# S5 tables in another layout, weights rounded one unit earlier, and other planner costs in a one-core decoder trunk

## The chip, the cores and the metric

The kernel runs on one core of a Trainium2 chip. The metric is device time in microseconds (us), the median of three runs. TensorE (PE) does the matmuls, VectorE (DVE), ScalarE (ACT) and GpSimd (POOL) the rest, and SyncE (SP) issues most DMAs. POOL and ACT issue DMAs too, in order with their other instructions.

## The reference

One decoder layer over 512 tokens of width 1024, in float32. Three token mixers run side by side on the normalised input: a gated linear recurrence (LRU, branch a), chunked gated linear attention (GLA, branch b) and a complex diagonal state space (S5, branch c). They are merged by sigmoid gates; cross attention to 256 memory tokens and a SwiGLU follow, each with a residual and a layer norm.

```python
proj = h @ w_in + b_in
u_lru, g_lru, q, k, v, og, lr, u_s5, gate_logits = jnp.split(proj, IN_SPLITS, axis=-1)
y_a = rg_lru(causal_dwconv(u_lru, ...), ...) * gelu(g_lru)
y_b = rms_norm(gla_chunked(q, k, v, log_f), gla_norm_g) * silu(og)
z = gelu(s5_ssm(u_s5, ...)); y_c = z * sigmoid(z @ s5_w_glu + s5_b_glu)
gates = sigmoid(gate_logits.reshape(B_, L, N_BRANCH, D_MODEL))
merged = sum(gates * einsum('blnw,nwd->blnd', ys, w_branch), axis=2)
h = layer_norm(DN_ALPHA * h + merged @ w_mix_out, ln1_g, ln1_b)
h = layer_norm(DN_ALPHA * h + cross_attention(h, mem, ...), ln2_g, ln2_b)
h = layer_norm(DN_ALPHA * h + swiglu(h, w_gu, w_down), ln3_g, ln3_b)
# s5_ssm, for 32 groups of 16 channels with 64 complex states each:
mag = exp(lam_re * dt); ab = mag * (cos(lam_im * dt) + i sin(lam_im * dt))
x[t] = ab * x[t-1] + (f * b) u[t];   y[t] = Re(c x[t]) + d u[t]
```

## The kernel before

**Tiles.** Activations lie transposed, features on the 128 partitions and all 512 tokens along a row; a `heap` tile is 128x512 float32 (52 buffers). Each matmul is done in three passes to keep float32 accuracy: the weight is split into a rounded half `whi` (ACT copies `raw` to fp32r) and a remainder `wlo` (DVE, `raw - whi`), the activation likewise into `..h` and `..l`, and `mm3` multiplies hi by hi, hi by lo and lo by hi. A weight unit is 128x1024 (512 KB), 162 of them are split so; one unit makes eight contraction blocks, 24 matmuls of 512 columns. `take(name)` (L248) hands out the next unit, splits units up to three ahead (`split_to`, L225) and issues DMAs three further (`dma_to`, L216). Raw and split units share one pool of 14 buffers.

**Stages.** Input layer norm (`ln_in`, L465) and the keys `kT`; the projections `us` (S5 input), `u`, `g`, `qk`, `lr`, `vo`; then, between the gate units `gt` and the branch projections `br`, the three mixers; `w_mix` and layer norm 1 (`proj_ln`, L1284); the memory values `xv` and queries `xq`; the heads (L1379); `w_xo` and layer norm 2; the first feed-forward units `f0` (first the tokens 0 to 255 of four units, then 256 to 511 of the same four); `fg`, `fu`; `w_dn` and layer norm 3.

**Order.** The program is written out when the kernel is built. Each engine runs its own list in order. Main work (projections) is straight code. The mixers, the layer norms of the token tiles and the heads are generators in the background (`start_bg`, L302). At each `slot()` (L278) the planner lets a generator write its next step if the clocks it keeps for DVE and ACT are less than `LEAD` ns ahead of its clock for PE, and if the tiles that the step names are ready by its own account (`_account`, L77). What an instruction costs in that account is in `pe_cost`, `dve_cost`, `act_cost`, `pool_cost` (L98 to L125). So these estimates decide the order of the instructions on every engine, and nothing else. A generator may hold at most three PSUM banks (`hold`, L263).

**S5.** `s5_prep` (L601) builds tables on POOL: the powers 0 to 7 of `ab` (`pw`), ordered by power and then group, the scaled `bb` and `bbs`, the eighth power of the phase (`wr`, `wi`), and `bz`. For each quarter q of the groups, `phasors(q)` (L716) makes the 64 phases per group (`phr`, `phi`) on POOL by doubling: five squarings of 128x8 (`sq`) and five complex products growing to 128x256. `s5a` (L753) has DVE make two `E` and two `C` stacks (each two products and a sum, the second product in `tm`), PE transpose `E` into `Et` and multiply `C` by `bz` into `G`, ACT copy `G` into `gx`, and POOL's DMA queue load `U` and route `gx` through memory into `Tz`. `s5b` then does `e = Et U` on PE, eight small matmuls put one by one behind the threes of the main work (`pump`), DVE's scan, and `y`. The merge of a branch is DVE's `th<-th,br`, which reads the branch's PSUM bank; the next use of the bank waits for it.

**Layer norm of a tile.** When `p` of a token tile is done, DVE adds the residual, ACT sums squares, POOL takes the power -1/2 (`st<-st,mh`), DVE scales (`lh`); PE transposes (`tp`), ACT and DVE round into `h1Th`, `h1Tl`. `xq` needs those of all four tiles.

Of the kernel before, what the change touches and what calls it, by code (L numbers as in the profile page):

```python
# [16 lines left out]
P = 128  # L17
# [22 lines left out]
AHEAD = 3  # L40
DMA_AHEAD = 3
NHEAP = 52
LOG = []
LEAD = 6500.0
# [7 lines left out]
class Plan:  # L52


    def __init__(self):
        self.written, self.read, self.dma = {}, {}, 0.0
# [5 lines left out]
class Engine:  # L62
# [14 lines left out]
    def _account(self, name, a, k):  # L77
        aps = [x for x in (*a, *k.values()) if hasattr(x, "free_size")]
        outs, ins = [aps[0]] + [x for x in [k.get("accum_out")] if x is not None], aps[1:]
        p = self._plan  # L80
        t = self.ns
        for x in ins:
            t = max(t, p.written.get(x.name, 0.0) + (HOP if name != "matmul" else 0.0))
# [3 lines left out]
        end = t + self._cost(self, name, a, k, aps)  # L87
        self.ns = end
# [9 lines left out]
def pe_cost(eng, name, a, k, aps):  # L98
    if name == "transpose":
        return 109.0  # L100
    rhs = k["rhs"]
    return rhs.free_size() / 2.4 if rhs.dtype == F32R else max(rhs.free_size() / 0.6, 110.0)


def dve_cost(eng, name, a, k, aps):
    n = max(x.free_size() for x in aps[:2])
    return 67.0 + n * {"memset": 0.5, "reciprocal": 6.0}.get(name, 1.0) / 0.96


def act_cost(eng, name, a, k, aps):  # L110
    if name != "activation":
        return 700.0
    ns = 60.0 + 0.83 * aps[0].free_size() + (200.0 if "accum_out" in k else 0.0)
    func = a[2]
    if func not in (AF.Copy, AF.Identity, AF.Square, AF.Abs) and func != eng.func:
        eng.func = func
        ns += 1300.0
# [3 lines left out]
def pool_cost(eng, name, a, k, aps):  # L121
    return 1100.0 if name == "dma_start" else 100.0 + 0.9 * aps[0].free_size()
# [7 lines left out]
def hybrid_kernel(ctx: ExitStack, tc: tile.TileContext, I, out, dbg=None):  # L130
# [17 lines left out]
    def H(s, dt=F32):  # L148
        return heap.tile([P, 512], dt, tag="h", name=nm(s))
# [64 lines left out]
    st = {"dma": 0, "split": 0}  # L214
# [10 lines left out]
    def split_to(n):  # L225
        while st["split"] < min(n, len(order)):
            i = st["split"]
            dma_to(i + 1)
            if i < NK32:
                st["split"] += 1  # L230
                continue
            name, _, size = order[i]
            if name == "w_lr":
# [3 lines left out]
                split(p3[:, 0], p3[:, 1], r3)  # L237
                splits[i] = pair
                st["split"] += 1
                continue  # L240
            hi, lo = W("whi", F32R), W("wlo", F32R)
            split(hi[:, :size], lo[:, :size], raws.pop(i)[:, :size])
            splits[i] = (hi, lo)
            st["split"] += 1
# [3 lines left out]
    def take(name, ahead=AHEAD):  # L248
# [3 lines left out]
        split_to(i + 1 + ahead)  # L252
        dma_to(min(st["split"], i + 1 + AHEAD) + DMA_AHEAD)
# [347 lines left out]
    def s5_prep(R):  # L601
# [978 lines left out]
```

## Time and profile before

| | |
|---|---|
| median of three runs | 1030.89 us (1029.96 to 1031.49) |
| profiled execution | 1030.58 us |
| its span | 1028.9 us |
| mean granted clock of PE | 0.986 |
| PE busy | 995.0 us, 97% |
| DVE, ACT, POOL busy | 539.4, 367.3, 232.9 us |

The span runs from the first to the last instruction that the profile shows; 1.7 us lie outside it. PE is busy nearly always, so what can be won without taking matmuls away is its idle time and the time in which it ran at the lower of its two clocks (1.2 instead of 2.4 GHz).

### The profile page before, as it was taken

The page shows a single profiled execution, that of the slowest core. Times are in us where ns is not written, and L with a number is a line of the kernel's source. Part 1 is how long each engine was busy: PE and PEld are TensorE (multiplying, and loading weights), DVE is VectorE, ACT ScalarE, POOL GpSimd, SP SyncE. Part 2 cuts the span into 40 slices and gives each one's busy share as a digit, 9 for nine tenths or more (in the row PEclk, how much of TensorE's full clock was granted, in tenths as well). Part 3 has the DMA queues.
Part 4 walks back from the last instruction along what each step waited for, and adds up shares of the span by engine and source line. Part 5 has one row for each costly group of instructions (what it writes and reads, how often), then busy time and mean ns, then how long its engine had stood idle before and what let it go on. Part 6 is the DMA issues. An engine that isn't in the chain of part 4 may idle for free. (4 is left out here: it accounts for less than half of the span.)

```text
span 1028.9 us, 12601 instructions
## 1 busy us (share of the span) xinstructions
PE 995.0 (97%) x4856; PEld 822.4 (80%) x4856; DVE 539.4 (52%) x857; ACT 367.3 (36%) x598; POOL 232.9 (23%) x465
## 2 busy tenths in 40 slices
PE   9999979998989799999999999999999999999996
PEld 7888757876878688888888887898888888888885
DVE  5625846887294654457594555833333332242316
ACT  5634357422233232553343443433322312331211
POOL 1489950083745700002010000200000000000001
PEclk9999989999999899999999999999999999999999
DMA  9932243212342344537232311353342222232202
GB/s 351 333 135 87 85 124 103 82 62 83 103 123 103 116 144 161 169 110 230 95 131 96 123 42 62 110 198 110 126 123 98 97 102 103 93 112 93 92 20 83
DMA packets 38365, 123.76 MB, mean 120 GB/s; under 512 B 4865, under 2 KB 5281, under 8 KB 38305
## 3 DMA queue, kind: packets, MB, share of 16 engines
q1 hardware_dynamic: 29856, 97.79, 27.4%
q0 software_dynamic: 6592, 22.02, 6.8%
q10 hardware_dynamic: 1856, 3.15, 1.1%
q8 instruction: 38, 0.62, 0.3%
q14 instruction: 23, 0.18, 0.1%
HBM read 109.31 MB, written 11.53 MB: 117 GB/s over the span
## 5 line engine op out<-in xcount | busy, mean ns | idle before, releaser
L73 DVE TENSOR_TENSOR wlo<-raw,whi 128x1024 fp32r<-128x1024 f32 x162 | 197.9, 1228 | 220.7 <-ACT whi L73 165.0
L73 ACT ACTIVATE whi<-raw 128x1024 fp32r<-128x1024 f32 x162 | 168.4, 1055 | 63.7 <-DVE wlo L73 42.4
L73 PE MATMUL p<-whi,act 128*128 128x512 f32 x352 | 108.6, 389 | 0.0
L73 POOL TENSOR_TENSOR st<-st,mh 128x1 f32<-128x1 f32 x16 | 15.5, 970 | 396.2 <-DVE st L73 396.2
L73 PE MATMUL gt<-h0Th,whi 128*128 128x512 f32 x192 | 79.6, 415 | 7.8 <-DVE th L73 7.8
L73 PEld LDWEIGHTS p<-whi,act 128*128 128x128 f32 x352 | 66.1, 188 | 13.7
L73 PE MATMUL gt<-h0Tl,whi 128*128 128x512 f32 x192 | 76.5, 398 | 0.0
L73 PE MATMUL gt<-h0Th,wlo 128*128 128x512 f32 x192 | 76.3, 397 | 0.0
L73 PE MATMUL p<-wlo,act 128*128 128x512 f32 x176 | 68.5, 389 | 0.0
L73 PE MATMUL fg<-h2Th,whi 128*128 128x512 f32 x160 | 62.3, 389 | 0.0
L73 PE MATMUL fg<-h2Tl,whi 128*128 128x512 f32 x160 | 62.3, 389 | 0.0
L73 PE MATMUL fg<-h2Th,wlo 128*128 128x512 f32 x160 | 62.2, 389 | 0.0
L73 PE MATMUL fu<-h2Th,whi 128*128 128x512 f32 x160 | 62.2, 389 | 0.0
L73 PE MATMUL fu<-h2Tl,whi 128*128 128x512 f32 x160 | 62.2, 389 | 0.0
L73 PE MATMUL fu<-h2Th,wlo 128*128 128x512 f32 x160 | 62.2, 389 | 0.0
L73 ACT ACTIVATE th<-gt,gbh 128x512 f32<-128x512 f32 x24 | 16.5, 688 | 121.1 <-PE gt L73 100.5
L73 PEld LDWEIGHTS gt<-h0Th,whi 128*128 128x128 f32 x192 | 37.1, 193 | 14.7 <-DVE th L73 8.0
L73 ACT ACTIVATE sl<-fg 128x512 f32<-128x512 f32 x20 | 12.0, 598 | 99.4 <-PE fg L73 99.4
L73 PEld LDWEIGHTS gt<-h0Th,wlo 128*128 128x128 f32 x192 | 37.0, 193 | 8.1
L73 PEld LDWEIGHTS gt<-h0Tl,whi 128*128 128x128 f32 x192 | 37.1, 193 | 6.5
L73 DVE TENSOR_TENSOR sl<-sl,fu 128x512 f32<-128x512 f32 x20 | 13.7, 687 | 52.7 <-PE fu L73 52.7
L73 PE MATMUL p<-whi,oT 128*128 128x512 f32 x128 | 40.6, 391 | 0.0
(349 smaller groups left out, 2224.1 us busy)
## 6 DMA issues: line engine op xcount, KB each, us to landing
raw<-in_w_gu SPq DMA_DIRECT2D x44, 512.0 KB, 3.3
raw<-in_w_dn SPq DMA_DIRECT2D x22, 512.0 KB, 3.2
raw<-in_w_xk SPq DMA_DIRECT2D x8, 512.0 KB, 6.8
raw<-in_w_gatea SPq DMA_DIRECT2D x8, 512.0 KB, 3.2
raw<-in_w_gateb SPq DMA_DIRECT2D x8, 512.0 KB, 3.5
raw<-in_w_gatec SPq DMA_DIRECT2D x8, 512.0 KB, 3.3
raw<-in_w_xv SPq DMA_DIRECT2D x8, 512.0 KB, 4.3
raw<-in_w_mix SPq DMA_DIRECT2D x8, 512.0 KB, 3.9
```

The costliest lines, as they stand in the source:

```text
L73: return f(*a, **k)
```

## The change

Three things are changed.

1. *S5 tables.* `pw` and the stacks are ordered by group, then channel, then power, so that DVE's products write rows without a stride; before they wrote with a stride of eight elements. `phasors(q)` is no longer a doubling: once, two tables of eight powers per group are made for all 32 groups (`tables`: eight squarings of 128x32 and four complex products of 128x64 or 128x128), and a quarter is their outer product, six operations of 128x512 and the sign. `bz` is made per quarter by DVE (a memset and two copies), not by POOL.
2. *Weights.* `whi` of a unit is written one unit earlier than its `wlo` (`EARLY`), by `hi_to`.
3. *Planner.* The cost estimates are others, `LEAD` is 7000 ns.

The diff, cut to what is spoken of below:

```diff
@@ -38,10 +38,11 @@
 NBUF_W = 14
 NPAIR = 5
 AHEAD = 3
+EARLY = 1
 DMA_AHEAD = 3
 NHEAP = 52
 LOG = []
-LEAD = 6500.0
+LEAD = 7000.0
 NWARM = 2
...
-            t = max(t, p.written.get(x.name, 0.0) + (HOP if name != "matmul" else 0.0))
+            t = max(t, p.written.get(x.name, 0.0) + HOP)
...
-            end = p.dma + 1800.0
+            end = p.dma + (2000.0 if len(aps[0].ap) < 3 and len(aps[1].ap) < 3 else 4000.0)
+        elif name in ("matmul", "transpose"):
+            end += 165.0
...
+    n = rhs.free_size()
+    return n / 2.4 + 13.0 if rhs.dtype == F32R else max(n / 0.6 + 26.0, 180.0)
...
-    return 67.0 + n * {"memset": 0.5, "reciprocal": 6.0}.get(name, 1.0) / 0.96
...
+    return (n + 151.0) / 0.96 + (180.0 if "accum_out" in k else 0.0)
...
+
+    def hi_to(n):
+
+        while st["hi"] < min(n, len(order)):
+            i = st["hi"]
             dma_to(i + 1)
+            st["hi"] += 1
             if i < NK32:
-                st["split"] += 1
                 continue
...
+                hi = W("whi", F32R)
+                his[i] = (hi[:, :size], None, raws.pop(i)[:, :size], hi)
+            A.activation(his[i][0], his[i][2], AF.Copy)

+    def split_to(n):
+        while st["split"] < min(n, len(order)):
+            i = st["split"]
+            hi_to(i + 1)
+            st["split"] += 1
...
+            V.tensor_tensor(lo, raw, hi.bitcast(F32), ALU.subtract)
...
+        hi_to(i + 1 + ahead + EARLY)
...
-        pr, pi = (pw[0][:, 256 * m:256 * m + 256].rearrange("p (d g) -> p d g", g=32) for m in range(2))
-        pt = w[:, 384:512].rearrange("p (d g) -> p d g", g=32)
-        E.tensor_copy(pr[:, 0], abr)
-        E.tensor_copy(pi[:, 0], abi)
+        pr, pi = (pw[0][:, 256 * m:256 * m + 256].rearrange("p (g d) -> p g d", d=8) for m in range(2))
+        pt = w[:, 384:512].rearrange("p (g d) -> p g d", d=4)
+        E.tensor_copy(pr[:, :, 0], abr)
+        E.tensor_copy(pi[:, :, 0], abi)
         for k in (1, 2, 4):
-            s4 = [P, k, 32]
-            cmul(pr[:, k:2 * k], pi[:, k:2 * k], pr[:, 0:k], pi[:, 0:k],
-                 pr[:, k - 1:k].to_broadcast(s4), pi[:, k - 1:k].to_broadcast(s4), pt[:, 0:k])
+            s4 = [P, 32, k]
+            cmul(pr[:, :, k:2 * k], pi[:, :, k:2 * k], pr[:, :, 0:k], pi[:, :, 0:k],
+                 pr[:, :, k - 1:k].to_broadcast(s4), pi[:, :, k - 1:k].to_broadcast(s4), pt[:, :, 0:k])
...
+        def square(n):
+
+            (sr, si), (qr, qi) = sq[(n - 1) % 3], sq[n % 3]
+            mul(qr, sr, sr)
+            mul(tmp, si, si)
+            E.tensor_tensor(qr, qr, tmp, ALU.subtract)
+            mul(qi, sr, si)
+            E.tensor_tensor(qi, qi, qi, ALU.add)
+            return qr, qi
+
+        tabs = []
+
+        def tables():
+
+            for n in range(1, 4):
+                one_ = square(n)
+                yield 0
+            ft = H("ft").rearrange("p (g d) -> p g d", d=16)
+            for j in range(2):
+                t = H("pq")
+                rr, ii = (t[:, 256 * m:256 * m + 256].rearrange("p (g d) -> p g d", d=8) for m in range(2))
+                E.memset(rr[:, :, 0:1], 1.0)
+                E.memset(ii[:, :, 0:1], 0.0)
+                E.tensor_copy(rr[:, :, 1], one_[0])
+                E.tensor_copy(ii[:, :, 1], one_[1])
+                for k in (2, 4):
+                    one_ = square(3 * j + (4 if k == 2 else 5))
+                    s4 = [P, 32, k]
+                    cmul(rr[:, :, k:2 * k], ii[:, :, k:2 * k], rr[:, :, 0:k], ii[:, :, 0:k],
+                         one_[0].unsqueeze(2).to_broadcast(s4), one_[1].unsqueeze(2).to_broadcast(s4),
+                         ft[:, :, 0:k])
+                    yield 0
+                if j == 0:
+                    one_ = square(6)
+                tabs.append((rr, ii))
...
+            if not tabs:
+                yield from tables()
             tr, ti, tt = H("phr"), H("phi"), H("pht")
...
-            k = 2
-            while k < 64:
-
-                b = k // 2
-                cmul(sr, si, ar[:, :, b], ai[:, :, b], ar[:, :, b], ai[:, :, b], sx)
-                s3 = [P, 8, k]
-                cmul(ar[:, :, k:2 * k], ai[:, :, k:2 * k], ar[:, :, 0:k], ai[:, :, 0:k],
-                     sr.unsqueeze(2).to_broadcast(s3), si.unsqueeze(2).to_broadcast(s3), at[:, :, 0:k])
-                yield 0
-                k *= 2
+            sh = [P, 8, 8, 8]
+            v = [a.rearrange("p (t b a) -> p t b a", b=8, a=8) for a in (tr, ti, tt)]
+            lo = [a[:, 8 * q:8 * q + 8].unsqueeze(2).to_broadcast(sh) for a in tabs[0]]
+            hi = [a[:, 8 * q:8 * q + 8].unsqueeze(3).to_broadcast(sh) for a in tabs[1]]
+            mul(v[0], lo[0], hi[0])
+            mul(v[2], lo[1], hi[1])
+            E.tensor_tensor(tr, tr, tt, ALU.subtract)
+            yield 0
+            mul(v[1], lo[0], hi[1])
+            mul(v[2], lo[1], hi[0])
+            E.tensor_tensor(ti, ti, tt, ALU.add)
...
-        bzs = [H("bz"), H("bz")]
-        for m in range(2):
-            E.memset(bzs[m], 0.0)
-            z4 = bzs[m].rearrange("p (t e x) -> p t e x", e=2, x=32)
-            src = bb3[:, 16 * m:16 * m + 16].rearrange("p (t e) c -> p t e c", e=2)
-            for e in range(2):
-                E.tensor_copy(z4[:, :, e, 16 * e:16 * e + 16], src[:, :, e])
...
-        sh = [P, 4, 8, 16]
+        sh = [P, 4, 16, 8]
 
         def over_d(a, g0):
+            return a[:, g0:g0 + 4].unsqueeze(3).to_broadcast(sh)
+
+        def over_c(a, g0):
             return a[:, g0:g0 + 4].unsqueeze(2).to_broadcast(sh)
 
-        def over_c(a, g0):
-            return a[:, :, g0:g0 + 4].rearrange("p d g -> p g d").unsqueeze(3).to_broadcast(sh)
-
         def stack(s, x, y, px, py, g0, op):
 
             o, tm = H(s), H("tm")
-            o4, t4 = (t.rearrange("p (g c d) -> p g d c", d=8, c=16) for t in (o, tm))
+            o4, t4 = (t.rearrange("p (g c d) -> p g c d", d=8, c=16) for t in (o, tm))
...
-            bz = R["bz"][q // 2][:, (q % 2) * 256:(q % 2) * 256 + 256]
-            yield (T, R["bz"][q // 2], *Es, *Cs)
+
+            bz = H("bz")
+            V.memset(bz[:, 0:256], 0.0)
+            zq = bz[:, 0:256].rearrange("p (t x) -> p t x", x=64)
+            src = R["bb"][0][:, 8 * q:8 * q + 8].rearrange("p (t e) c -> p t e c", e=2)
+            for e in range(2):
+                V.tensor_copy(zq[:, :, 48 * e:48 * e + 16], src[:, :, e])
+            yield (T, bz, *Es, *Cs)
```

The number of matmuls (4321 rows on PE's list) and SP's list stay the same. POOL's list shrinks from 457 rows to 259, DVE's grows from 822 to 830. What moves most is where S5 stands. On PE, before, the `e` of the first quarter stands between the matmuls of the first `vo` unit:

```order
L73 MATMUL vo_1422<-whi_1246,h0Th_164 128x512
L73 MATMUL vo_1422<-wlo_1247,h0Th_164 128x512
L73 MATMUL vo_1422<-whi_1246,h0Tl_166 128x512
L73 MATMUL e_1376<-U_1330,EtT_1318 128x64
L73 MATMUL vo_1423<-whi_1246,h0Th_164 128x512
L73 MATMUL vo_1423<-wlo_1247,h0Th_164 128x512
L73 MATMUL vo_1423<-whi_1246,h0Tl_166 128x512
```

In the changed kernel the `vo` unit has no `e` in it, and `Et`, `G` and `e` of that quarter come after GLA's attention, `e` between the products of branch a:

```order
L74 MATMUL vo_1375<-wlo_1250,h0Th_164 128x512
L74 MATMUL vo_1375<-whi_1173,h0Tl_166 128x512
L74 MATMUL vo_1372<-whi_1173,h0Th_164 128x512
L74 MATMUL vo_1372<-wlo_1250,h0Th_164 128x512
...
L74 MATMUL br_2070<-ya_1757,whi_1668 128x512
L74 MATMUL br_2070<-ya_1756,wlo_1708 128x512
L74 MATMUL e_2069<-U_1968,EtT_1956 128x64
L74 MATMUL br_2070<-ya_1794,whi_1668 128x512
```

So this `e` moved by about 340 rows of PE's list. On DVE, around the layer norm of the last token tile after `w_mix` (`lh` its result, `wlo` weight remainders, `h1Tl` the rounded transposes that `xq` reads), before:

```order
L73 SCALAR_TENSOR_TENSOR lt_4489<-res_4118,st_4136,lnp_4175 128x512
L73 SCALAR_TENSOR_TENSOR lh_4501<-lt_4488,st_4136,lnp_4173 128x512
L73 SCALAR_TENSOR_TENSOR lh_4503<-lt_4489,st_4136,lnp_4177 128x512
L73 TENSOR_TENSOR wlo_4508<-raw_4299,whi_4507 128x1024
L73 TENSOR_TENSOR wlo_4530<-raw_4511,whi_4529 128x1024
L73 TENSOR_TENSOR wlo_4548<-raw_4513,whi_4547 128x1024
L73 TENSOR_TENSOR h1Tl_4131<-tp_4565,h1Th_4129 128x4x128
L73 TENSOR_TENSOR h1Tl_4132<-tp_4572,h1Th_4130 128x4x128
L73 TENSOR_TENSOR wlo_4580<-raw_4515,whi_4579 128x1024
L73 TENSOR_TENSOR h1Tl_4131<-tp_4597,h1Th_4129 128x4x128
```

In the changed kernel two remainders and the rounding of the third tile (the first pair `h1Tl`) come ahead of that layer norm, and two more remainders and the `vx` behind it come ahead of the last `h1Tl`:

```order
L74 TENSOR_TENSOR wlo_4321<-raw_4130,whi_4319 128x1024
L74 TENSOR_TENSOR wlo_4343<-raw_4323,whi_4325 128x1024
L74 TENSOR_TENSOR h1Tl_3962<-tp_4361,h1Th_3960 128x4x128
L74 TENSOR_TENSOR h1Tl_3963<-tp_4368,h1Th_3961 128x4x128
L74 TENSOR_TENSOR st_3967<-st_3967 128x1
...
L74 SCALAR_TENSOR_TENSOR lh_4388<-lt_4375,st_3967,lnp_4004 128x512
L74 SCALAR_TENSOR_TENSOR lh_4390<-lt_4376,st_3967,lnp_4008 128x512
L74 TENSOR_TENSOR wlo_4392<-raw_4327,whi_4345 128x1024
L74 TENSOR_TENSOR wlo_4410<-raw_4329,whi_4394 128x1024
L74 TENSOR_TENSOR vx_4429<-xv_4317,vx_4428 128x512
L74 TENSOR_TENSOR vx_4433<-xv_4318,vx_4432 128x512
L74 TENSOR_TENSOR h1Tl_3962<-tp_4436,h1Th_3960 128x4x128
```

The layer norm moved behind the third tile's `h1Tl`; on PE the transposes `tp` of the third tile moved 12 rows earlier, those of the last did not move. On ACT, at the start of the kernel (`lj` belongs to the input layer norm of the last tile), before:

```order
L73 ACTIVATE kT_261<-kT_170 128x512
L73 DMA kT_263<-kT_261 128x512
L73 ACTIVATE lj_277,st_276<-x_99 128x512
L73 ACTIVATE lj_277,st_276<-x_100 128x512
```

and after:

```order
L74 ACTIVATE kT_261<-kT_170 128x512
L74 DMA kT_263<-kT_261 128x512
L74 ACTIVATE whi_265<-raw_168 128x1024
L74 ACTIVATE lj_279,st_278<-x_99 128x512
L74 ACTIVATE lj_279,st_278<-x_100 128x512
```

One `whi` moved ahead of the layer norm's sums. Last, the `tp` of the last tile of layer norm 2 stands 48 rows later on PE's list, directly ahead of the first matmul of `f0` on tokens 256 to 511, with its `h2Tl` behind it on DVE.

## Rows read from the trace of the kernel before

**Rows 1.** Page, part 1: busy time, share of the span and instructions of each engine.

```profile
PE 995.0 (97%) x4856; PEld 822.4 (80%) x4856; DVE 539.4 (52%) x857; ACT 367.3 (36%) x598; POOL 232.9 (23%) x465
```

**Rows 2.** Waits of PE: waiter, awaited: us in total, times, longest us.

```profile
PE gt L73 <- DVE th L73: 7.8, 2, 4.8
PE e L73 <- DMA U<-ud: 6.0, 1, 6.0
PE G L73 <- DVE C L73: 5.6, 1, 5.6
...
PE Et L73 <- DVE th L73: 0.9, 1, 0.9
```

**Rows 3.** Timeline of PE, 145 to 153 us: start, us, form, [idle before].

```profile
145.26 0.66 PE L73 MATMUL e<-U,EtT 128*128 128x64 f32 x2 [5.97 <-DMA U<-ud]
...
151.60 0.33 PE L73 MATMUL e<-U,EtT 128*128 128x64 f32 x2
...
152.52 0.33 PE L73 MATMUL e<-U,EtT 128*128 128x64 f32 x2
```

**Rows 4.** Timeline of PE, 249 to 254 us.

```profile
249.68 0.67 PE L73 MATMUL gt<-h0Th,whi 128*128 128x512 f32 x1 [4.79 <-DVE th L73]
...
253.44 0.40 PE L73 MATMUL gt<-h0Th,whi 128*128 128x512 f32 x1
```

**Rows 5.** Timeline of PE, 306 to 312 us.

```profile
306.33 0.80 PE L73 MATMUL gt<-h0Th,whi 128*128 128x512 f32 x1 [3.00 <-DVE th L73]
...
311.48 0.40 PE L73 MATMUL gt<-h0Th,whi 128*128 128x512 f32 x1
```

**Rows 6.** Timeline of PE, 352 to 357 us.

```profile
352.78 1.22 PE L73 MATMUL br<-yb,whi 128*128 128x512 f32 x2
...
356.05 0.40 PE L73 MATMUL br<-yb,wlo 128*128 128x512 f32 x1
```

**Rows 7.** Timeline of POOL at 139 us.

```profile
139.03 0.98 POOL L73 DMA_DIRECT2D U<-ud  x1
```

**Rows 8.** Groups of DVE by form: xcount | busy us, mean ns | idle before.

```profile
L73 DVE TENSOR_TENSOR E<-bb,pw 128x512 f32<-128x512 f32 x8 | 10.0, 1246 | 0.0
```

**Rows 9.** Timeline of DVE, at 114 and at 349 us.

```profile
113.77 0.69 DVE L73 TENSOR_TENSOR E<-E,tm 128x512 f32<-128x512 f32 x1
...
349.49 1.08 DVE L73 TENSOR_TENSOR tm<-bc,pw 128x512 f32<-128x512 f32 x1 [6.14 <-POOL phi L73]
```

**Rows 10.** Groups of POOL by form.

```profile
L73 POOL TENSOR_TENSOR s5w<-s5w 128x32 f32<-128x32 f32 x17 | 11.5, 677 | 0.8
...
L73 POOL TENSOR_SCALAR phi<-phi,sgn 128x512 f32<-128x512 f32 x4 | 6.1, 1515 | 0.4
...
L73 POOL TENSOR_TENSOR bb<-bb,bt 128x512 f32<-128x512 f32 x1 | 2.2, 2154 | 0.1
...
L73 POOL TENSOR_TENSOR bt<-bc,s5w 128x512 f32<-128x512 f32 x2 | 2.1, 1054 | 0.0
```

**Rows 11.** Groups of ACT by form.

```profile
L73 ACT ACTIVATE whi<-raw 128x1024 fp32r<-128x1024 f32 x162 | 168.4, 1055 | 63.7 <-DVE wlo L73 42.4 <-issue 5.8 <-PE f L73 5.1
...
L73 ACT ACTIVATE th<-gt,gbh 128x512 f32<-128x512 f32 x24 | 16.5, 688 | 121.1 <-PE gt L73 100.5 <-POOL phi L73 20.5
```

**Rows 12.** Timeline of DVE, 529 to 534 us.

```profile
529.47 0.16 DVE L73 TENSOR_TENSOR st<-st 128x1 f32<-128x1 f32 x1
...
532.42 1.42 DVE L73 SCALAR_TENSOR_TENSOR lh<-lt,st,lnp 128x512 f32<-128x512 f32 x2 [0.44 <-POOL st L73]
```

**Rows 13.** Timeline of PE, 526 to 541 us.

```profile
526.42 0.39 PE L73 MATMUL xv<-whi,memT 128*128 128x512 f32 x1
...
540.23 0.50 PE L73 MATMUL xq<-h1Tl,whi 128*128 128x512 f32 x1 [0.22 <-DVE h1Tl L73]
```

**Rows 14.** Timeline of DVE, 657 to 659 us.

```profile
657.55 1.28 DVE L73 TENSOR_TENSOR h2Tl<-tp,h2Th 128x512 fp32r<-128x512 f32 x2
```

**Rows 15.** DMA issues: KB each, median us from issue to landing.

```profile
raw<-in_w_gu SPq DMA_DIRECT2D x44, 512.0 KB, 3.3
```

More of the change, by code (lines that the diff above doesn't have):

```diff
@@ L55, in __init__ @@
     def __init__(self):
-        self.written, self.read, self.dma = {}, {}, 0.0
+        self.written, self.read, self.dma, self.lost, self.seq, self.life = {}, {}, 0.0, {}, 0, {}
     def ready(self, aps):
@@ L87, in _account @@
         end = t + self._cost(self, name, a, k, aps)
+        p.lost[self._cost.__name__] = p.lost.get(self._cost.__name__, 0.0) + t - self.ns
         self.ns = end
@@ L116, in act_cost @@
         eng.func = func
-        ns += 1300.0
+        ns += 1283.0
     return ns
 def pool_cost(eng, name, a, k, aps):
-    return 1100.0 if name == "dma_start" else 100.0 + 0.9 * aps[0].free_size()
+    if name == "dma_start":
+        return 800.0
+    if ALU.pow in a:
+        return 1100.0
+    return 300.0 + aps[0].free_size() * {"memset": 0.75, "tensor_copy": 1.2}.get(name, 2.1)
 def sp_cost(eng, name, a, k, aps):
@@ L148, in H @@
     def H(s, dt=F32):
-        return heap.tile([P, 512], dt, tag="h", name=nm(s))
+        t = heap.tile([P, 512], dt, tag="h", name=nm(s))
+        plan.life[t.name] = [plan.seq, plan.seq, nslot[0]]
+        return t
     def H8(s, dt=F32R):
@@ L223, in dma_to @@
             st["dma"] += 1
-    def split_to(n):
-        while st["split"] < min(n, len(order)):
-            i = st["split"]
+    his = {}
+    def hi_to(n):
+        while st["hi"] < min(n, len(order)):
+            i = st["hi"]
             dma_to(i + 1)
+            st["hi"] += 1
             if i < NK32:
-                st["split"] += 1
                 continue
@@ L236, in split_to @@
                 r3 = raws.pop(i)[:, :size // 2].rearrange("p (k c) -> p k c", c=16)
-                split(p3[:, 0], p3[:, 1], r3)
-                splits[i] = pair
-                st["split"] += 1
-                continue
[L241 to L244, printed above, removed]
+                his[i] = (p3[:, 0], p3[:, 1], r3, pair)
+            else:
+                hi = W("whi", F32R)
[6 more added lines that the diff above has]
+            st["split"] += 1
+            if i < NK32:
+                continue
+            size = order[i][2]
+            hi, lo, raw, whole = his.pop(i)
+            if lo is None:
+                low = W("wlo", F32R)
+                lo = low[:, :size]
+                splits[i] = (whole, low)
+            else:
+                splits[i] = whole
+            V.tensor_tensor(lo, raw, hi.bitcast(F32), ALU.subtract)
     nxt = [0]
@@ L737, in phasors @@
             E.tensor_scalar(ti, ti, sgn, -1.0, ALU.mult, ALU.mult)
             return tr, ti
[L741 to L749 removed]
+        R.update(bb=(bb3, bbs3), c=(c1, c2), p=(pr, pi), pe=(per, pei), ph=phasors, mag8=mag8)
@@ L1490, in hybrid_kernel @@
     assert nxt[0] == len(order)
+    LOG.append(("life", plan.life))
+    LOG.append((nslot[0], ("end", round(T.ns), {k: round(v) for k, v in plan.lost.items()})))
 def _layout(inputs):
```

53 lines of the change are left out of this document (28 added, 25 removed).

## The prediction

> **What bounds the kernel now.** I read the page's busy times first, then the list of waits of PE, then PE's timeline around each long wait, and last DVE and POOL at the same places. The busy times say that PE works 97% of the span [rows 1]: no edit here takes a matmul away, so only PE's idle time and the time at its lower clock can be won. The list of waits says where the idle time is: one wait of 6.0 us of `e` for the DMA of `U`, two of `gt` for DVE's `th` (7.8 in all), one of 5.6 of `G` for DVE's `C`, and 0.9 of `Et` for `th` [rows 2]. That is 5.97 + 7.8 + 5.6 + 0.9 = 20.3 us. All lie between 139 and 352 us, and all hang on S5.
>
> Behind each wait PE runs cold. After the 5.97 us, four groups of one `e` pair and three `vo` take from 145.26 to 151.60, 6.34 us; the next such group takes 152.52 - 151.60 = 0.92. Four at that price are 3.68, so 2.7 are lost [rows 3]. A warm matmul of 512 columns is thus about 0.23 us. Nine `gt` from 249.68 to 253.44 take 3.76 instead of 2.07: 1.7 lost [rows 4]. Twelve from 306.33 to 311.48 take 5.15 instead of 2.76: 2.4 [rows 5]. Eight `br` from 352.78 to 356.05 take 3.27 instead of 1.84: 1.4 [rows 6]. Together 8.2 us. The whole prize is 20.3 + 8.2 = 28.5 us.
>
> Why these waits exist: POOL's doubling for the first quarter ends only at 139.03, and the load of `U` stands behind it on POOL's queue [rows 7]; `e` waits for that load. At 349 us DVE's `tm` had waited 6.14 us for POOL's `phi` [rows 9], and behind it came the `C` that `G` wanted. ACT's `th` lost 20.5 us to `phi` as well [rows 11]: heap buffers held by a phasor on POOL. The two `gt` waits are for a `th<-th,br` queued on DVE behind S5 stacks and GLA's work.
>
> **The change part by part.**
>
> *Phasors.* A quarter falls from five squarings and products to six 128x512 products and a sign. The nearest rows are 1.05 us for a product of that size on POOL, 2.15 at worst, and 1.5 for the sign [rows 10]: 6 x 1.05 + 1.5 = 7.8, at most 6 x 2.15 + 1.5 = 14.4 us. The tables are made once: 40 operations of 32 columns, 24 of 64 or 128 and 8 small ones. The row for 32 columns says 0.68 [rows 10], so at that price for all 72 the tables cost 49 us at the most. Even if they began only where the old doubling ended, the first quarter would be done by 139 + 49 + 14 = 202 at the latest. Its `e`, 342 rows later on PE's list, now comes at about 233 us of PE's time. So POOL is off PE's path for this quarter by 31 us or more, and the 5.97 with its 2.7 go. For later quarters a phasor holds POOL, and its three heap buffers in the making, for 8 to 14 us; the 6.14 of DVE and the 20.5 of ACT lose their cause.
>
> *Stacks.* The 32 strided products, four groups of eight, take about 1.2 us; the row of one group says 1.25 [rows 8]. A sum of the same size, without a stride, also with two inputs in on-chip memory, took 0.69 in the same microseconds, while POOL was busy [rows 9]. I take 0.69 for the new products: 32 x 0.53 = 17 us less on DVE, 4.2 per quarter; the bounds are 0 and 17. DVE gains `bz`, one memset and two copies of 128 columns or 256 each quarter, under 3 x 0.69 = 2.1 us, so its work in a quarter falls by 2 to 4 us net of that.
>
> The Trainium skill, SBUF — State Buffer, section "Who interferes with whom", speaks against this: a DVE instruction with two inputs in SBUF takes its second through the read interface that it shares with GpSimd. By that the 1.2 us would be POOL's reads and not the stride, and the new products would stay slow wherever phasors run beside them. The rows speak for the stride: the 0.69 us sum has two such inputs too. By the page alone the sum would be that of the second rival below.
>
> *Order.* `Et` and `G` of the first quarter now stand behind GLA's attention and `e` in branch a. Following the lists of PE, DVE, ACT and POOL from there with the durations above, I find that each merge `th` ends 1 to 3 us before its bank is wanted again, and that only the last quarter's `G` (its `C` and `bz` 1 to 2 us early) and `e` are tight. So the 7.8, 5.6 and 0.9 go, with the other 5.5 cold us. If that cover is missing, one wait of 3 to 5.6 with 1.4 to 2.4 cold comes back.
>
> *Weights.* A `wlo` on DVE no longer waits for its `whi`. PE waited for that nowhere for long, so it gains nothing by itself. What it costs: a `whi` (1.06 us [rows 11]) stands ahead of the last input layer norm on ACT, and the chain DVE, `tp`, `kT` behind it is already what PE waits on there: +1.0 (0 to 1.5). The pool of 14 is full with one more half alive; each buffer that a `wlo` wants is freed at the latest by the unit before, and SP asks for `raw` units ahead, while a load takes 3.3 us [rows 15].
>
> *Layer norm 1.* The last tile's chain (from `st` at 529.47 to the end of `lh` at 533.84, 4.4 us [rows 12]) now starts only behind the third tile's `h1Tl`. From `xv`'s start at 526.42 [rows 13]: 24 matmuls and the transposes end at 532.9; the two roundings of the third tile end on DVE at 534.3; the chain at 538.7; two `wlo` at 1.14 each and two `vx` at 0.6 follow, to 542.2; the first `h1Tl` of the last tile ends at 542.8. Before, the matmul that needs it started at 540.23: +2.6 us. Behind that wait: the row nearest in length is the 3.00 us one, with 2.4 cold; the bounds are 0 and 2.4, I take 2.4.
>
> *Layer norm 2.* The last `tp` stands directly ahead of the matmuls that need it. Rounding on ACT and DVE, at about 0.6 us each (DVE: 1.28 for two [rows 14]), are seen once, less the second `tp` beside them: +0.8 (0 to 2).
>
> *Sum.* 1030.6 - 28.5 + 1.0 + 2.6 + 2.4 + 0.8 = 1008.9 us, against the profiled execution's 1030.58; the median of the runs is 0.3 above that, which I leave out. So 1009.
>
> **The rivals.**
>
> 1. *The lists fit better than I count:* the waits go and layer norm 1 stays warm or hides. Then 1030.6 - 28.5 + 0 to 2 = 1002 to 1004. For it: the sums for 539 us rest on DVE running back to back. Against: the order does put 4.4 us of chain and 3.5 of other work ahead of `h1Tl`.
> 2. *The stride is not what costs, or waits come back:* the stacks stay at 1.2, DVE does 4.2 us more per quarter than I count, and the last quarter's `G`, with 1 to 2 us in hand, waits 2 to 3, one merge too, each with about 2 cold: 8 to 10 us back, 1017 to 1019. For it: slack of 1 to 2 us over 170 us of hand sums is little. Against: rows 9.
> 3. *The planner's order changes nothing:* other banks are awaited, three of four waits return: 1030.6 - 8.7 + 6.8 = about 1029. Against: the doubling on POOL, which lies behind three of the four, is gone.
> 4. *Slower:* the weight pool. With `whi` a unit early, the 14 buffers leave SP one raw unit less ahead; if a load then lands behind the time that ACT wants it, every unit gives PE a wait. The gain of 21.7 us over 162 units is 0.13 us a unit: from there on the change loses, and at 0.2 us a unit it costs 32, 1041 us. For it: the pool is full without a spare. Against: 3.3 us for a load against 5.4 for the 24 matmuls of a unit [rows 15], and several units ahead.
>
> **How the numbers follow.** The forecast (waits gone, layer norms cost something: 1004 to 1014) has 0.55; rival 1 has 0.12, rival 2 0.20, rival 3 0.06, rival 4 0.07. The range for 8 in 10 leaves out the last two and the ends of the first: 1002 to 1021. A change of under 0.2%, 2 us, can't be told from none here. Rival 3 splits between same and faster, rival 4 is slower: faster 0.88, same 0.05, slower 0.07.
>
> **What would show it.** In the new profile: no `e<-U` wait at `vo` and POOL busy at least 50 us less; the stacks `E`, `tm`, `C` at about 0.7 us; no `gt` wait for `th` above 1 us; a wait of about 2.8 us of `xq` for `h1Tl`, with matmuls at half clock behind it; 0.8 of `f` for `h2Tl`. The forecast is wrong if a wait over 3 us stands between 200 and 400 us, if the stacks stay over 1 us, or if PE waits for `whi` or `wlo` in the feed-forward part.

## The result and the profile after

The changed kernel takes 1004.49 us (median of 4 runs, 1003.36 to 1005.75) against 1030.43 (1029.54 to 1031.49): a ratio of 0.9748, 95% interval 0.9731 to 0.9765, or 25.9 us less. The profiled execution took 1004.38 us, its span 1002.7.

Busy times first, against [rows 1]:

```profile
PE 985.8 (98%) x4856; PEld 816.1 (81%) x4856; DVE 532.8 (53%) x869; ACT 368.7 (37%) x598; POOL 185.3 (18%) x281
```

PE is 9.2 us less busy with the same 4856 matmuls, so that part is mostly clock (0.996 over the span against 0.986); POOL is 47.6 us less busy; DVE only 6.6. The waits of PE (waiter, awaited: us in total, times, longest), against [rows 2]:

```profile
PE xq L74 <- DVE h1Tl L74: 2.8, 1, 2.8
...
PE tp L74 <- DVE h0Tl L74: 1.7, 1, 1.7
PE f L74 <- DVE h2Tl L74: 0.8, 2, 0.5
...
PE ox L74 <- ACT pT L74: 0.2, 1, 0.2
```

All four S5 waits are gone, and `xq` waits for layer norm 1 instead. What became of the cold stretch shows in the windows table of both kernels (columns: window, its us, then busy us and instructions of PE, PEld, DVE, ACT, POOL, the granted clock, DMA share, GB/s). Before:

```profile
200.00:360.00 160.00, 145.68 (x868) 118.99 (x867) 104.45 (x149) 46.83 (x110) 95.13 (x214) 0.95 0.30 98
```

After:

```profile
200.00:360.00 160.00, 160.00 (x1017) 132.89 (x1016) 114.79 (x183) 52.94 (x124) 49.30 (x45) 1.00 0.41 128
```

PE is never idle there now, its clock is full, and 149 more matmuls, not all of one size, fit into the same 160 us. POOL has half the work there. The first quarter's `e`, which waited 5.97 us at 145.26 [rows 3], now runs at 220.72 without a wait (timeline of PE):

```profile
220.72 0.33 PE L74 MATMUL e<-U,EtT 128*128 128x64 f32 x2
```

The new wait and its clock, which answers to [rows 13] (timeline of PE: start, us, form, [idle before]):

```profile
512.81 0.50 PE L74 MATMUL xq<-h1Tl,whi 128*128 128x512 f32 x1 [2.77 <-DVE h1Tl L74]
...
513.61 0.53 PE L74 MATMUL xq<-h1Tl,whi 128*128 128x512 f32 x1
513.93 0.63 PE L74 MATMUL xq<-h1Th,wlo 128*128 128x512 f32 x1
514.36 0.63 PE L74 MATMUL xq<-h1Th,whi 128*128 128x512 f32 x1
...
517.26 0.39 PE L74 MATMUL xq<-h1Tl,whi 128*128 128x512 f32 x1
```

Read the distance between starts. It is 0.43 us in the middle, the lower clock, and 0.22 behind 517.26, the upper one (the granted clock is 1.00 from 512.81 to 513.60, 0.53 from 514.0 to 517.3 and 1.00 again behind that). From 513.61 to 517.26 nine matmuls take 3.65 us; at 0.228 they would take 2.05, so 1.6 us are lost.

The stacks on DVE (groups by form: xcount | busy us, mean ns | idle before), against [rows 8]:

```profile
L74 DVE TENSOR_TENSOR E<-E,tm 128x512 f32<-128x512 f32 x8 | 9.2, 1146 | 0.3
...
L74 DVE TENSOR_TENSOR E<-bb,pw 128x512 f32<-128x512 f32 x8 | 6.8, 849 | 0.0
```

The product fell from 1246 ns to 849, not to 690, and the sum rose to 1146. The timeline of DVE says why. In a quarter with POOL idle, and then in one with the phasors beside it:

```profile
283.12 0.68 DVE L74 TENSOR_TENSOR E<-bb,pw 128x512 f32<-128x512 f32 x1
283.72 0.68 DVE L74 TENSOR_TENSOR tm<-bbs,pw 128x512 f32<-128x512 f32 x1
284.44 0.69 DVE L74 TENSOR_TENSOR E<-E,tm 128x512 f32<-128x512 f32 x1
```

```profile
211.39 3.44 DVE L74 TENSOR_TENSOR E<-E,tm 128x512 f32<-128x512 f32 x1
214.75 1.75 DVE L74 TENSOR_TENSOR E<-bb,pw 128x512 f32<-128x512 f32 x1
216.42 1.55 DVE L74 TENSOR_TENSOR tm<-bbs,pw 128x512 f32<-128x512 f32 x1
```

and POOL in the same microseconds:

```profile
213.20 1.06 POOL L74 TENSOR_TENSOR pht<-pq,pq 128x512 f32<-128x512 f32 x1
214.34 1.60 POOL L74 TENSOR_TENSOR phr<-phr,pht 128x512 f32<-128x512 f32 x1
```

A stack instruction takes 0.68 alone and 1.44 to 3.44 beside POOL's 128x512 products and sums. POOL pays as well, though not at first: its product at 213.20 takes 1.06 beside DVE's 3.44, no more than with DVE idle (1.07 at 254.06), but its sum at 214.34 takes 1.60, against 1.28 with DVE idle (255.21).

Where the 26.2 us of span came from, by landmarks of PE. The S5 input `us` starts at 39.13 (38.88): +0.25. `xq` starts at 509.53 (539.51, just ahead of the 540.23 of [rows 13]): -29.98, so the stretch with GLA and S5 gave 30.2. `f0` starts at 630.23 (657.53): +2.7 for layer norm 1 and the heads. `fg` starts at 656.85 (683.03): +1.1 for layer norm 2. 0.25 - 30.2 + 2.7 + 1.1 = -26.2.

### The profile page after: what moved, and what is told of

It reads as the page before. It is cut to its first block, busy times and chain, and to the rows that moved or that the text cites. A ratio compares the mean times of both kernels' runs of the same rounds, so it can differ in the third digit from the quotient of the medians.

```text
span 1002.7 us, 12403 instructions
## 1 busy us (share of the span) xinstructions
PE 985.8 (98%) x4856; PEld 816.1 (81%) x4856; DVE 532.8 (53%) x869; ACT 368.7 (37%) x598; POOL 185.3 (18%) x281
```

## The experiments

The forecast held, but for which reason? My theory was that POOL's doubling makes the S5 waits, and that relieving POOL and shortening the stacks removes them. The rivals: it is the planner's new order, or the earlier `whi`. I split the change into its three parts, then the S5 part into its own. An edit can work by itself or by the order that the planner then makes, so it matters which lists stay as they were (counted in the traces). The layout alone and both runs with the stride put back leave the lists as they were, but for two of PE's 4856 rows in the first. The S5 part alone moves some 150 of these rows; the new estimates, and EARLY in either kernel, move some 500 to 570. For those, an effect is that of the edit and its order together.

**S5 part alone.** The kernel before with the new table layout, the outer product and `bz` made on DVE; old weights, old estimates. The diff runs from the kernel before to this one.

```diff
-        sh = [P, 4, 8, 16]
+        sh = [P, 4, 16, 8]
...
-            ar, ai, at = (a.rearrange("p (t c) -> p t c", c=64) for a in (tr, ti, tt))
...
+            mul(v[0], lo[0], hi[0])
+            mul(v[2], lo[1], hi[1])
...
+            bz = H("bz")
+            V.memset(bz[:, 0:256], 0.0)
```

> The kernel before with the S5 part of the change alone (tables by group, outer-product phasors, bz on DVE); weights and planner costs as before, so e of the first quarter still stands in the first vo unit, at about 139 us. Theory A (the new order took away the wait of e, the relief of POOL and DVE the other three): the wait of e stays at 6 to 7.5 us with 2.7 cold, since in the changed kernel POOL ended the first phasors at 140.6 us, no earlier than before; the waits near 245, 303 and 346 us are gone or under 1 us. 1030.4 - 14.3 - 5.5 + 1 = about 1012 us (1009 to 1017). Rival B (the order alone closed the gaps, the tables only make POOL idle): three of four waits stay, 1024 to 1030. Rival C (the tables alone did all): under 1006.

Measured: 1004.43 us, ratio 0.9752 [0.9737, 0.9766]; the whole change gives 0.9748. That is rival C; the wait of `e` that theory A kept did not come. No S5 wait is left; the only long wait is new and earlier (timeline of PE, then of DVE):

```profile
100.95 0.77 PE L73 MATMUL g<-h0Th,wlo 128*128 128x512 f32 x1 [2.02 <-DVE wlo L73]
...
142.77 0.33 PE L73 MATMUL e<-U,EtT 128*128 128x64 f32 x2
```

```profile
90.79 0.79 DVE L73 TENSOR_TENSOR E<-bb,pw 128x512 f32<-128x512 f32 x1 [10.84 <-POOL pw L73]
...
99.58 1.31 DVE L73 TENSOR_TENSOR wlo<-raw,whi 128x1024 fp32r<-128x1024 f32 x1
```

DVE stood 10.84 us before the first stack for POOL's `pw`, and the `wlo` that `g` wants stood behind the stacks. One part does all the work of the three, in nearly the old order.

**Estimates alone.** The kernel before with the new cost functions and lead time.

```diff
-LEAD = 6500.0
+LEAD = 7000.0
...
-    return 1100.0 if name == "dma_start" else 100.0 + 0.9 * aps[0].free_size()
...
+    return 300.0 + aps[0].free_size() * {"memset": 0.75, "tensor_copy": 1.2}.get(name, 2.1)
```

> The kernel before with the new planner estimates and LEAD 7000 alone; old doubling on POOL, strided stacks, weights as before. e of the first quarter moves to PE row 888. Theory A: the wait of e goes (8.7 us with its cold part), but POOL still takes some 35 us for each phasor, so waits of DVE or ACT for phi stay and PE waits 5 to 12 us somewhere between 200 and 400 us; layer norm 1 gets its 2.8 us wait, since the order of its last tile comes from these estimates. 1030.4 - 8.7 + 3 and up to 6 less: 1016 to 1025. Rival B: 1004 to 1010. Rival C: 1026 or more.

Measured: 1060.53 us, 1.0292 [1.0277, 1.0307]: 30 us slower. Theories A and B are far off; only rival C's open "1026 or more" holds it, and that names no cause. The waits of PE:

```profile
PE y L73 <- DVE Xs L73: 14.8, 2, 14.2
PE glu L73 <- ACT z L73: 7.7, 1, 7.7
PE ybT L73 <- DVE ob L73: 4.9, 2, 2.9
```

ACT does wait long for phasors, 15.05 us before an `es` and 10.79 before a `whi`, but these waits end at 254.76 and 345.11, and the last `phi` is done by 378.6. The two longest waits of PE end at 445.48 and 462.48, in the last quarter of S5. There its `es` starts on ACT at 433.08, behind a `yt` that hangs on DVE and a DMA (timeline of DVE):

```profile
430.76 0.75 DVE L73 SCALAR_TENSOR_TENSOR yt<-ur,pc,yt 128x512 f32<-128x512 f32 x1 [8.82 <-DMA yt<-yd]
```

So the longest waits are for S5's last chain itself, with nothing put beside it on PE's list. That the phasors made it late is not shown.

**The change without the earlier `whi`.**

```diff
-EARLY = 1
+EARLY = 0
```

> The changed kernel with EARLY = 0: whi is written with its wlo again. Theory A (the rounding ahead of time gains nothing and costs the 0.7 us more at the start): tp waits 0.95 us for h0Tl instead of 1.65, the 2.8 us of xq stay; 1004.5 - 0.7 = 1003.8 (1002.5 to 1005.5). Rival D (a wlo that waits for its whi holds up DVE between the S5 stacks and the merges): new waits of gt for th between 200 and 400 us, 1007 to 1012.

Measured: 1023.60 us, 0.9935 [0.9920, 0.9949]: 19.1 us more than the change, above both theories. The waits of PE, and the longest in the timeline:

```profile
PE G L74 <- ACT th L74: 4.8, 1, 4.8
...
PE glu L74 <- ACT z L74: 2.1, 1, 2.1
PE br L74 <- DVE th L74: 2.0, 1, 2.0
```

```profile
264.03 1.11 PE L74 MATMUL G<-C,bz 128*32 128x128 f32 x16 [4.81 <-ACT th L74]
```

The `th` that it waits for stands on ACT directly behind two `whi`, 2.02 us (timeline of ACT):

```profile
261.38 2.02 ACT L74 ACTIVATE whi<-raw 128x1024 fp32r<-128x1024 f32 x2
263.28 0.70 ACT L74 ACTIVATE th<-gt,gbh 128x512 f32<-128x512 f32 x1
```

PE idles 11.6 us more than in the change, of which `G` 4.8, `glu` 2.1, `br` 2.0 and `ybT` 1.4 are 10.3, and is busy 7.4 us longer with the same matmuls (993.2 against 985.8; the granted clock of the span is 0.989 against 0.996). The two `whi` make 1.9 of the 4.81 us; before them ACT had waited 1.86 for DVE's `ob`. That EARLY does such a rounding a unit sooner, and so not directly ahead of a `th`, is read from the order; I did not follow it for every one of these waits, and some 540 of PE's rows stand elsewhere without EARLY, so the rounding and the new order are not separated.

**The earlier `whi` alone**, the kernel before with EARLY.

```diff
+EARLY = 1
...
+        hi_to(i + 1 + ahead + EARLY)
```

> The kernel before with whi one unit ahead and nothing else. Theory A': rounding ahead takes one wait of DVE for ACT away (1.2 us before the merge at 249 us) and costs up to 1 us at the start; the four S5 waits stay: 1029 to 1032 us. Rival D': DVE's free wlo closes the two gt waits for th: 1018 to 1024 us.

Measured: 1032.46 us, 1.0023 [1.0014, 1.0033]. `e` waits 6.8 for `U`, `ybT` 5.0, `Et` 5.0. The `gt` waits for `th` did go, as rival D' had it, but in the new order others came for them. So the same edit, with the order that the planner makes of it, costs about 2 us with the old instructions and estimates and gives 19.1 with the new ones.

**Stride put back.** The change with its order, and the products written with the stride of before.

```diff
-            V.tensor_tensor(o4, over_d(x, g0), over_c(px, g0), ALU.mult)
...
+            o4, t4 = (v.rearrange("p g c d -> p g d c") for v in (o4, t4))
```

> The changed kernel with the same instructions in the same order on every engine; only the 32 products of the stacks walk channel-fastest again, so each writes with a stride of eight elements. Theory E (the stride costs): the products of the third and fourth quarter, beside which POOL is idle and which took 0.68 us, take about 1.1. Rival F (POOL's reads, not the stride, made them slow): they stay at 0.7. Either way the last quarter has about 2 us in hand before G, so that 8 x 0.4 = 3.2 us more gives PE a wait of at most 1.5 us there: 1004.5 to 1007 us by E, 1004.5 by F.

Measured: 1008.17 us (1004.84 to 1009.92), 0.9793 [0.9776, 0.9809]: 3.7 us more, just above theory E's range. A product and a sum group:

```profile
L74 DVE TENSOR_TENSOR E<-bb,pw 128x512 f32<-128x512 f32 x8 | 10.4, 1296 | 0.0
...
L74 DVE TENSOR_TENSOR E<-E,tm 128x512 f32<-128x512 f32 x8 | 8.1, 1009 | 0.3
```

The stride costs 0.45 us a product (1296 against 849), but the profiled run (1004.84, the fastest of its runs) shows the waits of the change and no others on PE: there is cover for it. Where the median loses its 3.7 us, that trace does not show.

**Stride put back in the S5 part alone**, where the stacks lie beside no large product of POOL's:

```diff
-            V.tensor_tensor(t4, over_d(y, g0), over_c(py, g0), ALU.mult)
...
+            o4, t4 = (v.rearrange("p g c d -> p g d c") for v in (o4, t4))
```

> The S5 part of the change alone (as tables_only, 1004.4 us), the same instructions in the same order, but the 32 products write with a stride of eight elements. By G the outer product on POOL does the work: 1004 to 1009 us, the products at 1.1 to 1.3 us. By H the waits of gt for th and of G for C come back: 1014 to 1025 us.

Measured: 1013.79 us, 0.9841 [0.9827, 0.9856], 9.4 above the S5 part alone and just below theory H's range. `g` waits 5.2 for `wlo` and `gt` twice for `th`, 3.6 in all. The groups, first contiguous and then strided:

```profile
L73 DVE TENSOR_TENSOR E<-bb,pw 128x512 f32<-128x512 f32 x8 | 5.6, 701 | 10.8 <-POOL pw L73 10.8
```

```profile
L73 DVE TENSOR_TENSOR E<-bb,pw 128x512 f32<-128x512 f32 x8 | 9.1, 1140 | 10.8 <-POOL pw L73 10.8
```

0.70 against 1.14: that is the stride with no large product beside it. Two `gt` waits for `th`, as in [rows 4, 5], come back with the stride alone, at 2.4 and 1.1 us instead of 4.8 and 3.0.

**Doubling put back**, in the S5 part alone: layout and `bz` new, phasors as before. The diff runs from the S5 part alone.

```diff
-            mul(v[0], lo[0], hi[0])
...
+                cmul(ar[:, :, k:2 * k], ai[:, :, k:2 * k], ar[:, :, 0:k], ai[:, :, 0:k],
```

> The S5 part of the change alone (as tables_only, 1004.4 us), but with the doubling of the kernel before for the phasors on POOL, 35 us a quarter; the stacks stay contiguous, bz stays on DVE. Theory G (POOL's relief closed the waits: U's load and DVE's and ACT's heap buffers hang on phi): the wait of e at 139 us comes back at 4 to 6 us with 2 to 3 cold, and DVE waits for phi again in the later quarters; 1014 to 1028 us. Theory H (the contiguous stacks closed them: 17 us less on DVE): at most the wait of e returns, 1004 to 1012 us.

Measured: 1002.56 us, 0.9729 [0.9715, 0.9744], below even theory H's range and 1.9 us below the S5 part alone. The two intervals touch, and the kernel before had medians of 1029.8 to 1030.7 beside these runs, so a step between two runs is sure to about 1 us: the outer product gave nothing here, and whether it cost anything is at the edge. This is the run against my reason. The load of `U` was issued 5.8 us earlier than in [rows 7], and `e` finds it there (timelines of POOL and of PE):

```profile
133.21 0.99 POOL L73 DMA_DIRECT2D U<-ud  x1
```

```profile
138.57 0.33 PE L73 MATMUL e<-U,EtT 128*128 128x64 f32 x2
```

**Only the layout**: tables by group and contiguous stacks; doubling and `bz` on POOL as before. The diff runs from the kernel with the doubling put back.

```diff
-            bz = H("bz")
...
+        bzs = [H("bz"), H("bz")]
+        for m in range(2):
+            E.memset(bzs[m], 0.0)
```

> The kernel before with the tables by group and the contiguous stacks alone: doubling and bz both on POOL, weights and planner as before. Theory H (the contiguous stacks close the three later waits): those stay away. bz puts some 3.3 us ahead of the doubling on POOL again, so e waits 4 to 6 us at 139 us with 2 to 3 cold: 1002.6 + 5 to 8 = 1007 to 1011 us. Theory I (bz on DVE matters more than that): 1012 or more. Theory J (bz's place is without effect): 1002 to 1004.

Measured: 1011.75 us, 0.9827 [0.9813, 0.9840], between theories H and I. All four waits are still there, each about half as long: `e` 2.80 us (5.97 before), `gt` 2.02 and 1.15 (4.79 and 3.00), `G` 2.98 (5.63). All lists but two rows of PE's are those of the kernel before, so this is the work of shorter instructions alone. DVE is 12.8 us less busy, and POOL 9.7, though none of its instructions is gone; its doublings are 10 us shorter (`sq`, `phr`, `phi` and `pht` together 108.3 instead of 118.3). The first, from the end of the memset of `gx` to the issue of `U`, takes 31.2 us instead of 35.2 (timelines of POOL and of PE):

```profile
135.33 0.98 POOL L73 DMA_DIRECT2D U<-ud  x1
```

```profile
141.81 0.41 PE L73 MATMUL e<-U,EtT 128*128 128x64 f32 x2 [2.80 <-ACT ea L73]
```

The profile puts this wait down to ACT's `ea`, which `e` does not read. It reads `U`, whose load landed at 141.67.

POOL makes `bz` at 99.91:

```profile
99.91 0.52 POOL L73 MEMSET bz<- 128x512 f32 x1
...
102.19 1.04 POOL L73 COPY bz<-bb 128x128 f32<-128x128 f32 x2
```

From 99.91 to 103.2 that is 3.3 us of POOL, and two heap buffers held through all of S5. Moving it is worth 9.2 us. ACT's `th` still waits 18.5 for `phi` here and DVE's `tm` 6.7, the latter directly ahead of the `C` that `G` wants; with `bz` on DVE neither waits (ACT's `EtT` waits 8.3 for `phi` instead).

**U loaded before the doubling**, on the kernel with doubling put back.

```diff
+            if q == 0:
+                U = H("U")
+                G.dma_start(U.rearrange("p (g c) -> p g c", c=64),
```

> tables_doubling (1002.6 us) with the load of the first quarter's U issued on POOL's queue ahead of the doubling instead of behind it; its data is long there. The 1.0 us wait of e goes, and nothing else moves: 1001.3 us (1000.8 to 1002.6).

Measured: 1001.96 us, 0.9731 [0.9717, 0.9744], the same as without. The 1.0 us wait of `e` that I meant to remove belongs to the last quarter (it is still there, at 342.71), not to the first: I had read a group for one instance.

**First stacks three slots later**, on the S5 part alone.

```diff
+            if q == 0:
+                yield -3
```

> tables_only (1004.4 us) with the first quarter's stacks written three slots later, so that DVE does four wlo first instead of waiting 10.8 us for POOL's pw. The 2.0 us wait of g for wlo and the slow matmuls behind it go: 1001.0 to 1002.5 us. If DVE's wait for pw did no harm beyond that, nothing else moves.

Measured: 1008.39 us, 0.9796 [0.9782, 0.9809], 4.0 worse than the S5 part alone. The `g` wait went, and the old `e` wait was under it:

```profile
143.78 0.66 PE L73 MATMUL e<-U,EtT 128*128 128x64 f32 x2 [5.32 <-DMA U<-ud]
```

There `U` is issued at 139.88, 2.2 us later than in the S5 part alone (137.71), and PE comes 4.3 us earlier (138.46 instead of 142.77). So in the S5 part alone the 2.0 us of `g` and the slow matmuls behind it made PE late enough for `U`. With the outer product the old order is too early for the first quarter; in the changed kernel, where `e` stands at 220.72, this can't happen.

**Two repairs of the change**: the last tile's layer norm written at once, and no early `whi` in the first eight units.

```diff
-        hi_to(i + 1 + ahead + EARLY)
+        hi_to(i + 1 + ahead + (EARLY if i >= 8 else 0))
...
+            if t == NT - 1 and not final:
+                es[-1][1] = next(es[-1][0])
```

> The changed kernel (1004.5 us) with two repairs: the last tile's layer norm after w_mix and w_xo is written at once, ahead of the weight remainders, and whi runs ahead only from the ninth unit on. The 2.8 us wait of xq falls to 0.2, the slow matmuls behind it (1.5 us) go, tp waits 0.95 instead of 1.65, f's second wait goes: 1004.5 - 2.6 - 1.5 - 0.3 - 0.6 = 999.5 us (998.5 to 1001.5).

Measured: 998.95 us (998.71 to 999.27), 0.9702 [0.9689, 0.9715], the fastest of all. The 2.77 of `xq` became

```profile
509.46 0.49 PE L74 MATMUL xq<-h1Th,whi 128*128 128x512 f32 x1 [0.35 <-ACT h1Th L74]
...
510.40 0.50 PE L74 MATMUL xq<-h1Tl,whi 128*128 128x512 f32 x1 [0.45 <-DVE h1Tl L74]
510.74 0.39 PE L74 MATMUL xq<-h1Th,wlo 128*128 128x512 f32 x1
510.97 0.40 PE L74 MATMUL xq<-h1Th,whi 128*128 128x512 f32 x1
```

with no cold matmuls behind, and the `tp` wait at the start fell from 1.7 to 1.0. The two repairs were not run apart.

**The repaired kernel with doubling**, which had been no worse under the old estimates.

```diff
-            mul(v[0], lo[0], hi[0])
...
+            while k < 64:
```

> change_ln_start (999.0 us) with the doubling of the kernel before for the phasors instead of the outer product; stacks, bz, weights, planner estimates and the two repairs stay. The planner now orders S5 otherwise (Et of the first quarter at PE row 736, its y ends at row 1624 instead of 1504). If what the outer product cost in tables_only (1.9 us against tables_doubling) is POOL's load on DVE alone: 996.5 to 999 us. If the outer product's place is to leave the planner slack (a phasor of 10 us on POOL instead of 35), waits of PE for S5 come back: 1002 to 1015 us.

Measured: 1031.37 us, 1.0008 [0.9999, 1.0017]: 32.4 us lost against the repaired change, far above both ranges. The waits of PE, and one of DVE:

```profile
PE o L74 <- DVE att L74: 8.9, 1, 8.9
PE ybT L74 <- DVE ob L74: 6.7, 2, 3.7
PE glu L74 <- ACT z L74: 4.1, 1, 4.1
```

```profile
DVE att L74 <- POOL att L74: 10.9, 1, 10.9
```

For the longest the path is plain: POOL's memset of `att` (222.78) stands on its queue directly behind the phasor of the second quarter, which took from 202.35 to 222.82; in the change it was done by 193.4, before that phasor. The other two were not followed.

## Why the prediction was right, and where it was not

One way through the medians, each step one edit: before 1030.4; layout and contiguous stacks 1011.8 (-18.7); `bz` to DVE 1002.6 (-9.2); outer product 1004.4 (+1.9); new estimates 1023.6 (+19.2); earlier `whi` 1004.5 (-19.1); the two repairs 999.0 (-5.5). The steps depend on their order: the outer product gains nothing under the old estimates (+1.9) and gives 32.4 under the new ones, repairs included.

*The prize.* Right. 28.5 us were forecast for the S5 stretch and 30.2 came: all four waits with their cold matmuls went. Of the 1.7 more, 1.4 are PE's busy time: in this stretch it fell by 9.6 us with the same matmuls, where the four cold stretches that were counted make 8.2. Of the forecast's signs of failure, a wait over 3 us between 200 and 400 us and a wait for weights in the feed-forward part are absent; the third, stacks over 1 us, is there for one group of six (`E` sums, 1.15). POOL fell by 47.6 us, where at least 50 was to show.

*Why these waits exist.* This step failed in part. The paths it named are in the traces. The wait of `e` follows the issue of `U` on POOL: issued at 139.03, 135.33 and 133.21 in three kernels with the doubling, `e` waits 5.97, 2.80 and nothing. And `tm`'s wait for `phi` stands ahead of `G` with the layout alone as it did before. What failed is the conclusion, that the doubling on POOL has to go for three of the four to go. With the doubling kept, all four are gone (1002.56), and the outer product on top gave nothing (1004.43). The layout, which shortens DVE's stacks and by 10 us also POOL's doublings beside them, and `bz` off POOL were enough: 18.7 and 9.2 us. In the S5 part alone the stride by itself makes 9.4. The prize came out right because all four waits went, by whichever cause; as to the cause it was luck.

*Phasors.* The sizes were right: on POOL a later quarter took 8.2 to 10.0 us (7.8 to 14.4 forecast), and the first was done at 140.6 (202 at the latest). But that is no earlier than the doubling was (139.03). What made it harmless was the place of `e` in the new order, as the step said, and in the S5 part alone a late PE.

*Stacks.* The stride was what costs when the stacks run alone, 1.14 against 0.70 us. But the saving was 9.6 us over the six groups, not 17, since in the new order a quarter's stacks run beside the phasors. The Trainium skill, SBUF — State Buffer, section "Who interferes with whom", which I set against the rows and then left, says that a DVE instruction with two inputs in SBUF contends with GpSimd's reads; the 3.44 us above agrees. The row that I took as proof, 0.69 beside a busy POOL [rows 9], stood beside products of 8 columns, and there DVE kept its time while some of POOL's took far longer (timeline of POOL of the kernel before):

```profile
112.55 1.09 POOL L73 TENSOR_TENSOR sq<-phi 128x8 f32<-128x8 f32 x1
113.72 0.20 POOL L73 TENSOR_TENSOR sq<-sq 128x8 f32<-128x8 f32 x1
```

Two operations of one size take 1.09 and 0.20. So the stride costs, and so does what POOL does beside it, and the second rival's time (1017 to 1019) did not come since there is cover: 1008.17 with the stride put back.

*Order.* Right for `e`: in the old order the outer product leaves a 5.3 us wait once PE is not held up before it (first stacks later), in the new one none. But the step judged the order only together with everything else: the estimates by themselves cost 30 us, and with the S5 part but without the earlier `whi` 19.2.

*Weights.* "It gains nothing by itself" is true in the kernel before (+2.0) and false in the changed one (-19.1). The step looked for PE waits on `wlo`, of which there were none above 0.2 us. It looked neither at what stands behind `whi` on ACT (a `th` that `G` waits for) nor at the order that the planner makes with EARLY. Its cost at the start was forecast at +1.0: `tp` waits 0.7 longer, and `us` starts 0.25 later. One profile can't tell that 0.25 from chance, since in the runs in which this `tp` waits 0.95 it starts anywhere from 30.96 to 32.31. The fourth rival, the weight pool, did not appear: PE waits for no `raw`, `whi` or `wlo` in the feed-forward part.

*Layer norm 1.* The wait was forecast at 0.22 + 2.6 = 2.8 and is 2.77. The cold behind it was forecast at 2.4 from the nearest wait in length and is 1.6. `xq` to `f0` grew by 2.7, less than 2.55 + 1.6 = 4.15, since 1.5 came back in the heads, of which the `ox` waits show 0.6 (1.0 before, 0.4 now) and a wait of `xq` for ACT that is gone 0.2; the rest I can't place.

*Layer norm 2.* +0.8 forecast, +1.1 measured.

*The sum.* Forecast 1009, measured 1004.5. The 4.5 us are 1.7 more from S5, 0.75 less at the start, and 2.3 less at layer norm 1 (5.0 against 2.7), less 0.3 at layer norm 2.

Still open: most of how the place of `bz` gives 9.2 us. The wait of `e` is 2.8 of it, and the slow groups behind that wait 1.6 (three of one `e` pair and three `vo` take 4.40 us from 141.81 to 146.21, at 0.92 they would take 2.76): `U` is issued 2.1 us earlier with `bz` on DVE. For `gt` and `G`, POOL's 3.3 us, the two held buffers and the slots that move with it were not separated. Nor was the earlier rounding separated from its order, and the S5 part with the earlier `whi` under the old estimates was not run.

## What to carry to other kernels

When several engines' waits surround a bound engine, finding a long job on the path of a wait does not show that this job has to go. Here the doubling could stay: 0.44 us less for each of DVE's products, with the lists as they were, and 3.3 us of other work taken off POOL's queue did it. So try the small relief on each engine by itself before the rewrite. A set of pacing estimates has no worth of its own: the same numbers cost 30 us with the kernel before, 19 with the S5 part in, and nothing net once the weights were also rounded earlier, so when instructions change, the order must be made and measured again with them. A wait that goes may have been hiding the next one (`g` over `e`), so a removed wait is worth the difference to what is late next.

## What the runs showed of the hardware

A 128x512 sum of two inputs took DVE 0.69 us alone and 3.44 beside POOL's products, which meanwhile took 1.08 and 1.06, as when DVE is idle; I had not expected a factor of 5. A write with a stride of eight elements took a DVE product from 0.70 to 1.14 us. Making DVE's products contiguous took 10 us off POOL's doublings, whose instructions and order stayed the same. After the 2.77 us wait PE's matmuls still started 0.23 us apart at first; the 0.43 us spacing began at 513.93, 1.1 us after work had resumed, and ended at about 516.9. Behind the 2.02 us wait of `g` in the S5 part alone it was there from the second matmul on (starts at 101.51, 101.94 and 102.36). So the cold stretch can begin well behind the wait; it cost 1.6 us here against 2.4 behind a wait of 3.00 [rows 5].
